# Shift and scale of the first three chunks computed by one-column matmuls in the start of a hybrid layer kernel

## The chip, the cores and the metric

The kernel runs on one core of a Trainium2 chip. Time is device time in microseconds (us) for one execution of the whole program. The engines are TensorE (PE; its weight loads are shown apart as PEld), VectorE (DVE), ScalarE (ACT), GpSimd (POOL) and SyncE (SP), which issues most of the transfers. Each engine runs its instructions strictly in the order of the program's listing for that engine, and they wait for each other through semaphores. The transfers named below are all issued from SP's one queue, at most eight of them outstanding.

## The reference

One layer on x of 1024 rows (S) by 1024 columns (D), in float32. The start, which the change touches, computes

```
c_act = silu(c)
mod   = c_act @ w_ada + b_ada          # 6 x 1024 columns
shift_t, scale_t, gate_t, shift_f, scale_f, gate_f = split(mod)
h     = x * (1 + scale_t) + shift_t
proj  = h @ w_in
```

The rest of the layer takes `proj` apart: a gated delta rule over 8 heads behind a short convolution, band attention over 16 heads, both projected and merged by gates, an output projection, a LayerNorm, then a second modulation, an up-projection, a convolution of width 3, a gated product, a down-projection and a second LayerNorm.

## The kernel before

Products of full precision are made of three products of the type fp32r: each operand is split into a high part (a cast) and a low part (the rest), and `hh·wh`, `hl·wh` and `hh·wl` are added up in one PSUM bank (`mm_fm`, L284). Plain float32 products, which the start uses too, run on TensorE as two passes, each a weight load and a multiply.

The program goes through a start stage, the delta-rule heads with the gates' projections between them, the attention, the branches' projections and the merge, the first LayerNorm, the up-projection (L1193, with fewer products by sums of blocks), the down-projection (L1497), and the last LayerNorm. A scheduler that simulates the engines decides the order of instructions on each engine; the source order of the calls is what it starts from. So a change in one place moves instructions in others.

The start stage makes h transposed, in 8 chunks of 128 of its columns, and multiplies each chunk at once with the first three blocks of weights of w_in (called k, g and q after what they produce):

- `ada_cols(j)` (L354 to L368) loads chunk j's 1024x128 columns of w_ada for the shift and for the scale, as four transfers of 256 KB in two tiles `wa`, then x's columns of the chunk (`load_x`, `xj`, 512 KB). On VectorE it multiplies each 128-row slab of w_ada by its entry of c_act (`csil`, one value a partition) and adds the eight up: `acc`, by one TENSOR_SCALAR (L363) and seven SCALAR_TENSOR_TENSOR (L365) of 128x256.
- On TensorE two products with a column of ones (L397, into `pmods`) add up acc over the partitions; ScalarE adds the bias (L400). That gives shift and scale as one value a partition.
- For each half of the rows: four transposes of x (L406) into one PSUM bank `px`; ScalarE makes h in float32 (L407) and its high part `hh` (L408) from it; GpSimd subtracts to the low part `hl` (L409).
- `dense_chunk` (L383) multiplies the chunk two behind the transposed one with the three weight blocks: 18 products of 512 columns a chunk.
- `first_weights` (L380) loads one weight block (`raw`, 512 KB, L185); ScalarE casts it to `wh` (L177), GpSimd subtracts to `wl` (L180).

Columns of two chunks ahead are loaded before the loop (`LEAD` is 2), k's weights behind chunk 0's loads and g's behind chunk 1's; q's come behind chunk 2's loads and three small loads (L344 to L350). When all chunks are multiplied, ScalarE takes the first finished product (L526) and the delta rule's first stage begins.

Of the kernel before, what the change touches and what calls it, by code (L numbers as in the profile page):

```python
# [12 lines left out]
ALU = mybir.AluOpType  # L13
# [4 lines left out]
P = 128  # L18
# [24 lines left out]
LAG0 = 2  # L43
PACC = 1
PTR = 0
G0 = 1
GA = (3, 2, 2, 2, 3, 2, 2, 99)
EP = (4,12)
# [105 lines left out]
def hybrid_layer(  # L154
# [182 lines left out]
        DVE.tensor_scalar(bb[:, :, m], vt[:, o:o + NK], float(m), None, ALU.add)  # L337

    pmods = pbank("pmods", "pm")
    accs, mark0 = {}, {}  # L340

    def ab_weights():
        raw = ring("rab", [P, NK, 16])
# [10 lines left out]
    def ada_cols(j):  # L354
        wa = [ring("wa", [P, 4, 2, P]) for _ in range(2)]
        for i in range(2):
            for m in range(2):
                SP.dma_start(wa[i][:, :, m, :],
                             w_ada2[4 * P * i:4 * P * i + 4 * P, m * D + j * P:m * D + j * P + P].rearrange(
                                 "(k p) n -> p k n", p=P))  # L360
        acc = accs[j] = ring("acc0", [P, 2, P])
        with tc.issue_after(mark0["acc"]) if mark0 and PACC else nullcontext():
            DVE.tensor_scalar(acc, wa[0][:, 0], csil[:, 0:1], None, ALU.mult)  # L363
            for k in range(1, NK):
                i = DVE.scalar_tensor_tensor(acc, wa[k // 4][:, k % 4], csil[:, k:k + 1], acc,  # L365
                                             ALU.mult, ALU.add)
        mark0["acc"] = i.ins
        return load_x(j)  # L368
# [9 lines left out]
    wfirst, pend = {}, {}  # L378

    def first_weights(m):  # L380
        wfirst[m] = wblock(kview(w_in2, first[m][0], P), NK)

    def dense_chunk(k):  # L383
        for m in first:
# [4 lines left out]

    xs = []  # L390
    for j in range(LEAD):
        xs.append(ada_cols(j))
        first_weights("kg"[j])
    for j in range(NK):
        pm = pmods[:, 2 * j:2 * j + 2]
        for m in range(2):
            PE.matmul(pm[:, m:m + 1], accs[j][:, m, :], ones[:, 0:1], start=True, stop=True)  # L397
        cs = ring("mc", [P, 2])
        for m in range(2):
            ACT.activation(cs[:, m:m + 1], pm[:, m:m + 1], AF.Identity, bias=bb[:, j, m:m + 1])  # L400
        h32 = ring("h32", [P, S])
        for n in range(2):
            N = slice(512 * n, 512 * n + 512)
            px = pbank(nm("px"), "px")
            for t in range(4):
                tr = PE.transpose(px[:, t * P:t * P + P], xs[j][:, 4 * n + t, :], ident)  # L406
            ACT.activation(h32[:, N], px, AF.Identity, bias=cs[:, 0:1], scale=cs[:, 1:2])  # L407
            ACT.activation(hh[:, j, N], px, AF.Identity, bias=cs[:, 0:1], scale=cs[:, 1:2])  # L408
            POOL.tensor_tensor(hl[:, j, N], h32[:, N], f(hh[:, j, N]), ALU.subtract)  # L409
        if j + LEAD < NK:  # L410
            xs.append(ada_cols(j + LEAD))
        if j == 0:
            wab, al, dtb = ab_weights()
            first_weights("q")
        if j == VJ:
            o = VO["b_gate"]
            vectors(o, [rows(b_gate[0]), rows(b_conv_ffn[0])])
            DVE.tensor_scalar(hbg, vt[:, o:o + 2 * NK], 0.5, None, ALU.mult)
            vectors(VO["conv_a"], [conv_a[0].rearrange("t (r p) -> (t r) p", p=P),
                                   norm_a, rows(ln1_g[0]), rows(ln1_b[0])])  # L420
            vectors(VO["conv_f"], [conv_ffn[0, 0:2].rearrange("t (r p) -> (t r) p", p=P)])
            vectors(VO["conv_f"] + 88, [rows(conv_ffn[0, 2])])
        if j >= LAG:
            with tc.issue_after(tr.ins) if PTR else nullcontext():
                dense_chunk(j - LAG)
# [1216 lines left out]
```

## Time and profile before

| | |
|---|---|
| median of 3 runs | 2221.73 us (2216.29 to 2221.82) |
| profiled execution | 2222.92 us |
| its span in the trace | 2221.2 us, granted TensorE clock 0.987 |
| busy: PE / DVE / ACT / POOL | 96% / 70% / 47% / 26% of the span |
| loads in the first 75 us | 32 of w_ada (256 KB), 8 of x and 6 of w_in (512 KB) |

A row of the timeline gives the start, the time, the engine, the source line, the operation, the output and inputs by the program's names, their shapes and a count; in brackets stands how long the engine was idle before it, and what ended that. Rows of the waits give engine, tile and line, what was waited for, and the sum, number and longest of the waits. A row of a group has the count, the busy time and the mean of one in ns, and the idle time before. The groups of one tile give the shortest, median and longest in ns. A line can be that of a helper that all engines' work of a kind shares (L177 and L180 split any operand).

### The profile page before, as it was taken

The page shows a single profiled execution, that of the slowest core. Times are in us where ns is not written, and L with a number is a line of the kernel's source. Part 1 is how long each engine was busy: PE and PEld are TensorE (multiplying, and loading weights), DVE is VectorE, ACT ScalarE, POOL GpSimd, SP SyncE. Part 2 cuts the span into 40 slices and gives each one's busy share as a digit, 9 for nine tenths or more (in the row PEclk, how much of TensorE's full clock was granted, in tenths as well). Part 3 has the DMA queues.
Part 4 walks back from the last instruction along what each step waited for, and adds up shares of the span by engine and source line. Part 5 has one row for each costly group of instructions (what it writes and reads, how often), then busy time and mean ns, then how long its engine had stood idle before and what let it go on. Part 6 is the DMA issues. An engine that isn't in the chain of part 4 may idle for free. (4 is left out here: it accounts for less than half of the span.)

```text
span 2221.2 us, 31629 instructions
## 1 busy us (share of the span) xinstructions
PE 2125.3 (96%) x11469; PEld 1776.9 (80%) x11469; DVE 1555.7 (70%) x3228; ACT 1037.9 (47%) x2216; POOL 588.5 (26%) x544
## 2 busy tenths in 40 slices
PE   6998999999999999999999999999899999999998
PEld 5687787777878787798989788888788878887876
DVE  8567585765667664467676653556998788879897
ACT  4645253434334334467675642235544444445453
POOL 4323232332322232233342522424011000000023
PEclk9999999999999999999999999999999999999999
DMA  9232333423233412211111424342242222253222
GB/s 286 80 112 78 91 94 107 119 74 108 85 91 93 142 36 82 79 57 51 60 55 65 154 91 137 105 152 86 67 161 95 86 76 83 89 209 133 95 95 86
DMA packets 228415, 224.68 MB, mean 101 GB/s; under 512 B 27482, under 2 KB 184595, under 8 KB 228259
## 3 DMA queue, kind: packets, MB, share of 16 engines
q1 hardware_dynamic: 228179, 222.63, 31.6%
q8 instruction: 90, 1.47, 0.3%
q14 instruction: 66, 0.54, 0.1%
q10 hardware_dynamic: 80, 0.03, 0.0%
HBM read 180.63 MB, written 48.28 MB: 103 GB/s over the span
## 5 line engine op out<-in xcount | busy, mean ns | idle before, releaser
L180 POOL TENSOR_TENSOR wl<-raw,wh 128x1024 fp32r<-128x1024 f32 x88 | 212.2, 2413 | 325.4 <-ACT wh L177 303.1
L1193 PE MATMUL pup<-hh,wop 128*128 128x512 f32 x704 | 225.2, 391 | 1.6 <-DVE wop L180 1.6
L1193 PE MATMUL pup<-t,wop 128*128 128x512 f32 x792 | 190.1, 393 | 3.3 <-ACT t L177 2.0
L1193 PEld LDWEIGHTS pup<-t,wop 128*128 128x128 f32 x792 | 148.2, 188 | 38.0 <-ACT t L177 2.4
L1193 PEld LDWEIGHTS pup<-hh,wop 128*128 128x128 f32 x704 | 132.0, 188 | 31.0 <-DVE wop L180 2.0
L177 ACT CAST wh<-raw 128x1024 fp32r<-128x1024 f32 x88 | 92.4, 1050 | 134.6 <-DMA raw<-in_w_in_dram 56.0
L1234 POOL TENSOR_TENSOR cc<-cc,G 128x512 f32<-128x512 f32 x22 | 44.6, 2028 | 375.9 <-DVE G L1216 311.7
L284 PE MATMUL pqkv<-hh,wh 128*128 128x512 f32 x352 | 143.1, 407 | 0.0
L284 PE MATMUL pqkv<-hl,wh 128*128 128x512 f32 x352 | 140.8, 400 | 0.0
L284 PE MATMUL pqkv<-hh,wl 128*128 128x512 f32 x352 | 139.8, 399 | 0.0
L1193 PE MATMUL pup<-hl,wop 128*128 128x512 f32 x352 | 137.5, 391 | 0.0
L663 DVE TENSOR_TENSOR FT<-FT,G 128x16 f32<-128x16 f32 (+30 forms) x248 | 120.9, 488 | 17.6 <-POOL G L608 10.3
L944 POOL TENSOR_SCALAR G<-G,FT 128x640 f32<-128x640 f32 (+4 forms) x103 | 69.9, 681 | 182.3 <-DVE FT L943 160.4
L177 ACT CAST wop<-wr 128x512 fp32r<-128x512 f32 x110 | 65.6, 620 | 99.1 <-DVE wr L1179 65.1
L284 PE MATMUL pgt<-hh,wl 128*128 128x512 f32 x240 | 95.1, 396 | 0.8 <-POOL wl L180 0.8
L284 PE MATMUL pgt<-hh,wh 128*128 128x512 f32 x240 | 95.4, 397 | 0.3 <-DVE tmp L530 0.3
L284 PE MATMUL pgt<-hl,wh 128*128 128x512 f32 x240 | 94.7, 395 | 0.0
L1497 PE MATMUL pdn<-hl 128*128 128x512 f32 x360 | 86.7, 395 | 3.9 <-DVE hl L180 2.4
L180 DVE TENSOR_TENSOR wop<-wr,wop 128x512 fp32r<-128x512 f32 x110 | 80.2, 733 | 13.3 <-ACT wop L177 12.4
L963 DVE TENSOR_TENSOR pl<-pp,ph 128x512 fp32r<-128x512 f32 (+2 forms) x116 | 72.5, 635 | 17.4 <-ACT ph L962 16.6
L1497 PEld LDWEIGHTS pdn<-hl 128*128 128x128 f32 x360 | 68.5, 191 | 19.2 <-DVE hl L180 2.8
L941 ACT ACTIVATE G<-G,FT 128x640 f32<-128x640 f32 (+4 forms) x103 | 71.6, 696 | 19.0 <-DVE FT L936 16.9
(457 smaller groups left out, 6127.8 us busy)
## 6 DMA issues: line engine op xcount, KB each, us to landing
raw<-in_w_in_dram SPq DMA_DIRECT2D x72, 512.0 KB
wr<-in_w_up_dram SPq DMA_DIRECT2D x44, 512.0 KB
raw<-in_w_ada_dram SPq DMA_DIRECT2D x32, 512.0 KB
dr<-g_d SPq DMA_DIRECT2D x18, 512.0 KB
dr<-in_w_down_dram SPq DMA_DIRECT2D x18, 512.0 KB
wa<-in_w_ada_dram SPq DMA_DIRECT2D x32, 256.0 KB
gates_d<-GT SPq DMA_DIRECT2D x32, 256.0 KB
g_d<-G SPq DMA_DIRECT2D x14, 512.0 KB
```

Source lines behind the costliest of these rows:

```text
L177: ACT.copy(h, src)
L180: return le.tensor_tensor(l, src, f(h), ALU.subtract).ins
L284: PE.matmul(ps, a[:, k, :], r[k][:, 512 * n:512 * n + 512], start=(k == 0 and a is wh and r is rh), stop=(k == NK - 1 and a is wl))
L663: DVE.tensor_tensor(pr[:, :, 0:i + 1], ft[:, :, 0:i + 1], fa[:, i:i + 1, 0:i + 1].to_broadcast([P, 8, i + 1]), ALU.mult)
L941: ACT.activation(sb[:, 0:n], sb[:, 0:n], AF.Exp, bias=mx[:, nb - 1:nb], scale=-1.0, accum_out=mx[:, 2:3])
L944: POOL.tensor_scalar(sb[:, 0:n], sb[:, 0:n], mx[:, 3:4], 0.0, ALU.mult, ALU.add)
L963: DVE.tensor_tensor(pl[:, B, :], pp, f(ph[:, B, :]), ALU.subtract)
L1193: PE.matmul(ps, a[:, u, k, :], b[v][k], start=(new and k == 0 and u == 0 and v == 0), stop=(k == 3 and u == 1), skip_group_check=not new)
L1234: self.later(7, lambda: POOL.tensor_tensor(o, o, self.t, ADD))
L1497: PE.matmul(sets[s_][i], a[:, u, i * P:i * P + P], b[:, v, :], start=(new and not seed and j == 0 and u == 0 and v == 0), stop=(j == len(q ...
```

## The change

For the first three chunks (`MP`) the sums on VectorE go. TensorE multiplies the slabs of w_ada out instead: slab k as the stationary operand, entry k of c_act as the one moving column, eight products for the shift and eight for the scale, accumulated in `pmods`. That is 48 products more (96 passes) and six products with ones fewer (12 passes). In the whole start stage, the low parts `hl` of the chunks and `wl` of the three first weight blocks are subtracted on VectorE instead of GpSimd. And the load of k's weights is called before chunk 0's columns, that of g's before chunk 1's.

```
+MP = 3
@@
-    accs, mark0 = {}, {}
+    accs, was, mark0 = {}, {}, {}
@@ ada_cols
+        was[j] = wa
+        if j < MP:
+            return load_x(j)
         acc = accs[j] = ring("acc0", [P, 2, P])
@@
     def first_weights(m):
-        wfirst[m] = wblock(kview(w_in2, first[m][0], P), NK)
+        wfirst[m] = wblock(kview(w_in2, first[m][0], P), NK, le=DVE)
@@
     for j in range(LEAD):
+        first_weights("kg"[j])
         xs.append(ada_cols(j))
-        first_weights("kg"[j])
     for j in range(NK):
         pm = pmods[:, 2 * j:2 * j + 2]
         for m in range(2):
-            PE.matmul(pm[:, m:m + 1], accs[j][:, m, :], ones[:, 0:1], start=True, stop=True)
+            if j < MP:
+
+                for k in range(NK):
+                    PE.matmul(pm[:, m:m + 1], was[j][k // 4][:, k % 4, m, :], csil[:, k:k + 1],
+                              start=(k == 0), stop=(k == NK - 1))
+            else:
+                PE.matmul(pm[:, m:m + 1], accs[j][:, m, :], ones[:, 0:1], start=True, stop=True)
@@
-            POOL.tensor_tensor(hl[:, j, N], h32[:, N], f(hh[:, j, N]), ALU.subtract)
+            DVE.tensor_tensor(hl[:, j, N], h32[:, N], f(hh[:, j, N]), ALU.subtract)
```

The scheduler also orders things anew. Below, numbers behind a name tell tiles of that name apart; they differ between the two programs.

ScalarE in the start, before: `wh_13` is the cast of g's weights, `wh_23` that of q's, `px_27` and `px_28` are the halves of a chunk's transposes; the first two px rows are chunk 1's first half and, behind the small L351, its second half.

```order
L177 CAST wh_13_161<-raw_15_163 128x1024
L400 ACTIVATE G_2_93<-pmods_122,G_2_93 128x1 x2
L407 ACTIVATE h32_26_221<-px_27_222,G_2_93 128x512
L408 ACTIVATE hh_84<-px_27_222,G_2_93 128x512
L351 ACTIVATE SB_1_92<-SB_1_92 128x8
L407 ACTIVATE h32_26_221<-px_28_230,G_2_93 128x512
L408 ACTIVATE hh_84<-px_28_230,G_2_93 128x512
L177 CAST wh_23_211<-raw_25_213 128x1024
```

ScalarE now, from chunk 0's first half (`px_17`) to chunk 1's first (`px_27`):

```order
L417 ACTIVATE h32_16_169<-px_17_170,G_2_93 128x512
L418 ACTIVATE hh_84<-px_17_170,G_2_93 128x512
L352 ACTIVATE SB_1_92<-SB_1_92 128x8
L178 CAST wh_23_201<-raw_25_203 128x1024
L417 ACTIVATE h32_16_169<-px_18_178,G_2_93 128x512
L418 ACTIVATE hh_84<-px_18_178,G_2_93 128x512
L410 ACTIVATE G_2_93<-pmods_122,G_2_93 128x1 x2
L417 ACTIVATE h32_26_225<-px_27_226,G_2_93 128x512
```

The cast of q's weights stood behind both halves of chunk 1; now it stands ahead of chunk 0's second half (`px_18`).

TensorE between the two halves of chunk 1's transposes, before: seven products with the weights of k (`wh_7`, `wl_8`) and g (`wh_13`).

```order
L406 MATMUL px_27_222<-ident_68,xj_12_159 128x128 x4
L284 MATMUL pfirst_39_292<-hh_84,wh_7_139 128x512
L284 MATMUL pfirst_40_299<-hh_84,wh_13_161 128x512
L284 MATMUL pfirst_40_299<-hl_85,wh_13_161 128x512
L284 MATMUL pfirst_41_300<-hh_84,wh_13_161 128x512
L284 MATMUL pfirst_39_292<-hl_85,wh_7_139 128x512
L284 MATMUL pfirst_39_292<-hh_84,wl_8_140 128x512
L284 MATMUL pfirst_41_300<-hl_85,wh_13_161 128x512
L406 MATMUL px_28_230<-ident_68,xj_12_159 128x128 x4
```

TensorE there now, with the three products ahead of the first half (`wh_23` and `wl_24` are q's weights, `wa_19` and `wa_20` chunk 2's slabs):

```order
L285 MATMUL pfirst_42_325<-hh_84,wh_23_201 128x512
L285 MATMUL pfirst_42_325<-hl_85,wh_23_201 128x512
L285 MATMUL pfirst_42_325<-hh_84,wl_24_202 128x512
L416 MATMUL px_27_226<-ident_68,xj_15_149 128x128 x4
L285 MATMUL pfirst_39_310<-hh_84,wh_4_123 128x512
L285 MATMUL pfirst_41_318<-hh_84,wh_10_137 128x512
L285 MATMUL pfirst_43_326<-hh_84,wh_23_201 128x512
L404 MATMUL pmods_122<-csil_109,wa_19_186 128x1 x4
L404 MATMUL pmods_122<-csil_109,wa_20_187 128x1 x4
L404 MATMUL pmods_122<-csil_109,wa_19_186 128x1 x4
L404 MATMUL pmods_122<-csil_109,wa_20_187 128x1 x2
L416 MATMUL px_28_234<-ident_68,xj_15_149 128x128 x4
```

Products with q's weights now stand ahead of chunk 1's transposes, and 14 of chunk 2's 16 one-column products between the halves.

VectorE now, in the middle of the stage: `h32_26` is chunk 1's h, `h32_32` chunk 2's, `h32_44` chunk 3's; `wa_47_354` and `wa_48_355` are the two tiles of chunk 5's columns, `wa_53_409` is the first of chunk 6's.

```order
L367 TENSOR_SCALAR G_2_93<-wa_47_354,csil_109 128x256
L419 TENSOR_TENSOR hl_85<-h32_26_225,hh_84 128x512
L369 SCALAR_TENSOR_TENSOR G_2_93<-wa_47_354,csil_109,G_2_93 128x256 x3
L369 SCALAR_TENSOR_TENSOR G_2_93<-wa_48_355,csil_109,G_2_93 128x256
L419 TENSOR_TENSOR hl_85<-h32_32_276,hh_84 128x512
L369 SCALAR_TENSOR_TENSOR G_2_93<-wa_48_355,csil_109,G_2_93 128x256 x3
L419 TENSOR_TENSOR hl_85<-h32_32_276,hh_84 128x512
L419 TENSOR_TENSOR hl_85<-h32_44_337,hh_84 128x512
L367 TENSOR_SCALAR G_2_93<-wa_53_409,csil_109 128x256
L369 SCALAR_TENSOR_TENSOR G_2_93<-wa_53_409,csil_109,G_2_93 128x256 x3
L419 TENSOR_TENSOR hl_85<-h32_44_337,hh_84 128x512
```

Before, no lower part of a chunk stood on VectorE; now they stand between the steps of later chunks' sums. On SP's queue the small vector loads (L314) and the next three weight blocks moved ahead of the second tile of chunk 5's columns or of the rest, and chunk 7's columns ahead of chunk 6's.

## The prediction

> **What bounds the kernel now.** I read the page's first part, then the busy time by stretches of the start, the waits there, and the timeline of single instructions.
>
> ```profile
> span 2221.2 us, 31629 instructions
> PE 2125.3 (96%) x11469; PEld 1776.9 (80%) x11469; DVE 1555.7 (70%) x3228; ACT 1037.9 (47%) x2216; POOL 588.5 (26%) x544
> ```
>
> TensorE is busy 96% of the span: over the whole program only its work and its waits count. The change touches the start alone, so that is read by itself (columns: stretch, its length, then busy time and instructions of PE, PEld, DVE, ACT and POOL, the granted clock, DMA share, GB/s).
>
> ```profile
> 0.00:21.50 21.50, 3.96 (x14) 2.85 (x14) 14.06 (x23) 7.19 (x12) 11.50 (x19) 1.00 0.95 273
> 20.00:23.00 3.00, 1.48 (x6) 1.38 (x7) 2.82 (x7) 0.41 (x2) 0.15 (x1) 1.00 0.41 49
> 24.00:26.00 2.00, 2.00 (x8) 1.61 (x7) 1.35 (x4) 1.45 (x3) 0.00 (x0) 1.00 1.15 345
> 26.00:43.00 17.00, 16.91 (x89) 13.91 (x88) 15.44 (x21) 9.41 (x18) 10.05 (x8) 1.00 1.15 343
> 43.00:45.00 2.00, 2.00 (x13) 1.61 (x12) 1.93 (x3) 1.13 (x2) 1.08 (x1) 1.00 0.24 62
> 45.00:49.00 4.00, 2.83 (x17) 2.19 (x16) 3.82 (x7) 1.59 (x5) 1.27 (x1) 1.00 0.90 255
> 49.00:56.00 7.00, 7.00 (x38) 5.62 (x37) 6.71 (x10) 4.08 (x8) 3.63 (x3) 1.00 1.06 309
> 58.00:66.00 8.00, 5.78 (x30) 3.43 (x30) 0.00 (x0) 2.29 (x6) 0.21 (x1) 1.00 0.01 3
> ...
> 73.40 0.69 ACT L526 ACTIVATE y<-pfirst,vt 128x512 f32<-128x512 f32 x1
> ```
>
> Three stretches: to 21.5 us TensorE waits for the first data and VectorE's sums; from then to 45 it is gapless, so what delays it there delays the end; from 45 to 66 it idles a little over 4 us in all (1.2 in 45 to 49, 2.2 in 58 to 66). The stage ends at 73.40, where ScalarE takes the first finished product. The waits that VectorE's sums cost TensorE:
>
> ```profile
> PE pmods L397 <- DVE G L365: 9.2, 4, 6.8
> PEld pfirst L284 <- POOL hl L409: 0.3, 1, 0.3
> ...
> 21.52 1.01 PE L397 MATMUL pmods<-ones,G 128*128 128x1 f32 x4 [6.78 <-DVE G L365]
> 46.99 0.61 PE L397 MATMUL pmods<-ones,G 128*128 128x1 f32 x4 [1.18 <-DVE G L365]
> 57.74 0.60 PE L397 MATMUL pmods<-ones,G 128*128 128x1 f32 x4 [0.98 <-DVE G L365]
> ```
>
> Of 9.2 us, 6.8 is chunk 1's wait before 21.52, which the change removes; the other two belong to chunks that keep their sums.
>
> **The change, step by step.** 1. *What replaces the 6.8 us.* After 21.52 the old order needs no q weights for some time: ScalarE casts them only behind chunk 1. In the new order the cast stands ahead of chunk 0's second half, on ScalarE's one queue, and TensorE's q products ahead of chunk 1's transposes. So the landing of the q weights decides.
>
> ```profile
> 19.97 0.43 SPq L185 DMA_DIRECT2D raw<-in_w_in_dram  x1
> 20.45 4.07 SPq L358 DMA_DIRECT2D wa<-in_w_ada_dram  x4
> ...
> 26.92 0.59 DVE L363 TENSOR_SCALAR G<-wa,csil 128x256 f32<-128x256 f32 x1 [1.53 <-DMA wa<-in_w_ada_dram]
> ```
>
> Chunk 3's first 512 KB of w_ada, right behind the q weights in the queue, ended a wait at 26.92. At 345 GB/s 512 KB take 1.5 us, so the q weights landed near 25.4. The change puts the same eleven blocks and the same three small loads ahead of them: I keep 25.4. The bounds: the data pause at 20 to 23 us (49 against 345 GB/s, 2.6 us, and some of the next) follows those small issues; without it 22.5; 26.9 at the latest. So the wait goes, and a later one takes its place.
>
> 2. *From the landing to chunk 1's second half.*
>
> ```profile
> 29.20 1.05 ACT L177 CAST wh<-raw 128x1024 fp32r<-128x1024 f32 x1
> 24.55 0.78 ACT L407 ACTIVATE h<-px,G 128x512 f32<-128x512 f32 x1 [1.56 <-PE px L406]
> 25.89 0.20 ACT L351 ACTIVATE SB<-SB 128x8 f32<-128x8 f32 x1
> 27.86 0.78 ACT L407 ACTIVATE h<-px,G 128x512 f32<-128x512 f32 x1 [1.76 <-PE px L406]
> L180 DVE TENSOR_TENSOR ob<-raw,ob 128x1024 fp32r<-128x1024 f32 x6 | 7.3, 1222 | 8.3 <-ACT ob L177 4.9 <-DMA ob_d<-ob 3.4
> 23.40 1.05 PE L406 MATMUL px<-ident,xj 128*128 128x128 f32 x4
> 25.96 0.63 PE L284 MATMUL pfirst<-hl,wh 128*128 128x512 f32 x1
> 26.39 0.63 PE L284 MATMUL pfirst<-hh,wl 128*128 128x512 f32 x1
> 29.50 0.40 PE L284 MATMUL pfirst<-hl,wh 128*128 128x512 f32 x1
> 29.74 0.39 PE L284 MATMUL pfirst<-hh,wl 128*128 128x512 f32 x1
> ```
>
> Cast 1.05: 26.45. Chunk 0's second half on ScalarE takes the 1.34 from 24.55 to 25.89: 27.8. Meanwhile VectorE subtracts the q low part: this shape costs it 1.22 on other tiles, to 27.7, and the third q product issues by 28.1. Chunk 1's transposes (1.05) end at 29.2. Three products follow. Products start 0.43 us apart at 26 us and 0.23 apart at 29.6, the granted clock being 1.00 in both rows: after 7 us of idling TensorE is slow, which that column doesn't show. It restarted at 21.52 and was fast between 26.39 and 29.5. In the new order it idles again until the cast at 26.45, so three products cost 1.3: 30.5.
>
> Then come 14 of chunk 2's 16 one-column products, each two passes of load and multiply: 28 passes. Before has such passes only with ones as moving column, in fours:
>
> ```profile
> 21.52 0.93 PEld L397 LDWEIGHTS pmods<-ones,G 128*128 128x128 f32 x4 [7.28 <-DVE G L365]
> 37.13 0.52 PEld L397 LDWEIGHTS pmods<-ones,G 128*128 128x128 f32 x4
> L397 PEld LDWEIGHTS pmods<-ones,G x32: 186/192/338, 9.9 to 58.1; 128*128 128x128 f32 x32
> 27.55 0.19 PEld L284 LDWEIGHTS pfirst<-hh,wh 128*128 128x128 f32 x1
> ```
>
> Less the last load's own time (0.338 slow, 0.19 fast), three steps take 0.59 and 0.33: 0.20 a pass slow, 0.11 fast. The first fast load stands at 27.55, 6.0 us after the restart; the last slow product 4.9 after. I take 6.0, so fast from 32.5: ten passes at 0.20, eighteen at 0.11, together 4.0, and 34.5. Chunk 1's second transposes (0.6) let ScalarE begin at 35.1, against 27.86: **+7.2**. Bounds of this term: 3.1 (all fast) to 5.6 us (all slow) for the 28 passes.
>
> The Trainium skill (TensorE: Matmul & The Clock Gate, Part 2, "LDWEIGHTS (loading the stationary operand)") prices a load by its columns over 1.2, in nanoseconds; for 128 that is 107 ns whatever the state, which agrees with the fast 0.11 and not with the slow 0.20. An estimate by that page is 28 x 0.107 = 3.0 us, and chunk 1's second half 1.0 earlier.
>
> 3. *What follows, to 73.40.* TensorE's remaining work is the same but for one product more done by then in the new order (twelve against eleven): −0.2. The waits of 1.18 and 0.98 should go, since TensorE comes 7 us later to the same sums: −2.2; they stay if the sums are as late (bound 0). Two new ones come from VectorE's queue, where a lower part stands behind a sum that waits for its data.
>
> ```profile
> L365 DVE SCALAR_TENSOR_TENSOR G<-wa,csil,G x56: 477/485/2506, 6.3 to 57.2; 128x256 f32<-128x256 f32 x56
> L180 DVE TENSOR_TENSOR hl<-dr,hl 128x512 fp32r<-128x512 f32 x54 | 35.9, 695 | 2.7 <-ACT hl L177 1.7 <-PE pdn L1497 1.0
> L409 POOL TENSOR_TENSOR hl<-h,hh 128x512 fp32r<-128x512 f32 x16 | 21.2, 1322 | 33.9 <-ACT hh L408 33.8
> L180 POOL TENSOR_TENSOR wl<-raw,wh 128x1024 fp32r<-128x1024 f32 x3 | 7.5, 2513 | 7.1 <-ACT wh L177 7.1
> ```
>
> Chunk 2's first lower part is queued behind chunk 5's fifth sum step. Its data is the tenth 512 KB after the q weights: 25.4 + 10 x 1.53 at 343 GB/s = 40.7, and the small vector loads, which before cost 1.6 of 43 to 45 and 1.0 of 45 to 49, now lie ahead of it: 43.4. With 0.5 for that step and 0.7 for the part it is ready at 44.6. TensorE wants it after 27 products of 0.23 and 20 passes of 0.1 to 0.11 from 34.8: near 43.0. So +1.6, bounds 0 (no pause) and 1.8. Behind it on VectorE wait the same chunk's second part and all later sums. Chunk 3's second part stands behind four steps of chunk 6's sum, whose data the new order of loads puts behind chunk 7's and three weight blocks: five blocks on, at 309 to 343 GB/s, near 51.4; with 1.9 for the steps and 0.7, 54.0 against TensorE's 52.6 to 53: +1.2, bounds 0 and 1.4. The last chunk's part takes VectorE 0.7 where it took GpSimd 1.3: −0.3 by the last product (−0.6 at most).
>
> The new waits end by the data, not by TensorE: up to 2.8 us more or less in step 2 is mostly taken up there.
>
> **The sum**: 7.2 − 0.2 − 2.2 + 1.6 + 1.2 − 0.3 = **+7.3 us**. Against the profiled execution (span 2221.2, with 1.7 around it 2222.9) that is 2230.2; that execution is 1.2 above the median, so on the median of 2221.7 I say **2229.0**.
>
> *Costed at nothing:* the 64 passes of chunks 0 and 1 (12.8 us at 0.20), the weights loaded ahead and the removed 24 sum steps: all lie before 25.4, under the wait for the q weights. If these landed at 22.5 the passes would still be done, w_ada of chunk 1 being the seventh block of twelve; were they not, each four cost 0.8. GpSimd's freed 28.7 us (21.2 + 7.5) buy nothing by themselves, its lower parts being waited for 0.3 us in sum; what they buy is VectorE's steps at 0.485 rather than up to 2.5 us, which is in the −2.2. After 73.40 the order differs in a few neighbouring rows, taken as zero.
>
> **Rivals.** *A: the pause in the data does not recur.* The q weights land at 22.5, TensorE restarts 2.9 earlier, and the rest goes as above: +4.4, **2226.1**. For it: the small loads' issue may overlap otherwise; against: it is the same queue in the same order.
>
> *B: TensorE stays slow through the one-column products*, which leave the array nearly empty. 28 passes at 0.20 cost 5.6 instead of 4.0, and some ten products after them at 0.43 instead of 0.23, 2.0: 3.6 more, **2232.6**, if the new waits stay as large because VectorE is late too; if their data comes as worked out, TensorE's lateness takes the place of their 2.8: 2229.8. For it: the fast pace came here after 5 us of 512-column work; against: fours of one-column passes stand amid it without harm. The Trainium skill (TensorE: Matmul & The Clock Gate, Part 4: PE-mode transpose) says that transposes do not count as TensorE's busy time for the clock gate; it says nothing of one-column products, and no row here shows one in a long run.
>
> *C, the other side: the delay is taken up again, and the kernel isn't slower.* Its place is 45 to 66 us, where TensorE idles 4.4 us in the old order; if all of that goes and neither new wait comes, the sum is 7.2 − 0.2 − 4.4 = +2.6, **2224.3**, and with A's landing −0.3, 2221.4. It decides if chunk 5's fifth step has its data by 41.7 and chunk 6's by 50.4 (the times TensorE wants the parts, less the steps). For it: 40.7 without the pause; against: the small loads stand ahead, and 2.2 of the idle time comes from ScalarE's last chunk, not from sums.
>
> That the change doesn't do what it says is out: the new order shows the products and the moved parts.
>
> **How the numbers follow.** My forecast 0.52, A 0.15, B 0.13, C 0.12, and 0.08 for a gain in rows after 73.40 that I can't see. My case's own range is 2226 to 2232: without the new waits −2.8, with the old ones kept +2.2. For 8 times in 10 it reaches into C and over B: 2220 to 2235. A measurement of this kernel tells 0.3% from no change, 6.7 us, so slower begins at 2228.4: three fifths of my case (0.31) and B, 0.44. Same: the rest of mine (0.21), A, and 0.11 of C, 0.47. Faster: the last 0.08 and 0.01 of C.
>
> **What would show it.** Right: ScalarE's q cast near 25.5, TensorE idle before it for 5 us or more, chunk 1's second half near 35, TensorE waiting for VectorE's lower parts near 43 and 53, the first finished product taken near 81. Wrong in step 1: the cast at 23; in step 2: chunk 2's passes 0.20 apart to their end; in step 3: no waits for lower parts. Wrong as a whole: ScalarE's first take at or before 76 us.

## The result, and the profile after

The changed kernel is slower by two thirds of a per cent.

| | before | after |
|---|---|---|
| median of 6 runs each | 2222.18 us (2216.29 to 2224.11) | 2234.76 us (2229.30 to 2238.34) |
| ratio, with its 95% interval | | 1.0065 (1.0053 to 1.0077) |
| profiled execution | 2222.92 us | 2233.64 us |
| first finished product taken | 73.40 us | 82.41 us |

The page's first part, after:

```profile
span 2231.9 us, 31777 instructions
PE 2146.4 (96%) x11553; PEld 1796.8 (81%) x11553; DVE 1543.5 (69%) x3223; ACT 1038.2 (47%) x2216; POOL 560.8 (25%) x525
```

TensorE is busy 21.1 us longer (2146.4 against 2125.3) in a span that is 10.7 us longer: it idles 10.4 us less and works 21.1 us more. A pass is one weight load and one multiply, two to each of the added products. The added passes are most of the 21.1 us (64 at 0.21 and 32 at 0.12 us, read below, make 17, less twelve that went); what is left is the same products done more slowly.

*Where the time goes, by stage.* The table gives, for each kernel's profiled execution, when TensorE begins the gates' products (soon after the start stage), and then the length of each later stage, between TensorE's first or last products of the neighbouring stages. "After, again" is the changed kernel's profiled execution beside a later group of runs; its median there was 2235.88 against 2219.50, a ratio of 1.0071 (1.0056 to 1.0086).

| | before | after | after, again |
|---|---|---|---|
| start, to the gates' first product | 80.6 | 89.5 (+8.9) | 89.9 (+9.3) |
| delta rule and gates | 550.0 | 552.9 (+2.9) | 552.4 (+2.4) |
| attention, branches | 737.7 | 739.1 (+1.4) | 742.1 (+4.4) |
| merge, up-projection | 615.2 | 615.2 | 615.0 |
| down-projection | 204.6 | 202.2 (−2.4) | 200.4 (−4.2) |

The start costs 9.0 us by the first finished product, and that repeats (82.80 again, +9.4). The rest of the +12.6 between the medians lies behind it.

*The start.* A dense product is one of the stage's 144 products of 512 columns; at the fast pace they start about 0.23 us apart, at the slow pace 0.43. Busy time by stretches, after; the columns are those of the prediction (PE, PEld, DVE, ACT, POOL, granted clock, DMA share, GB/s):

```profile
7.00:15.00 8.00, 7.55 (x36) 7.55 (x37) 1.59 (x3) 1.46 (x3) 0.00 (x0) 1.00 1.14 344
15.00:22.00 7.00, 7.00 (x36) 7.00 (x34) 0.92 (x2) 1.66 (x3) 0.46 (x1) 1.00 0.89 229
22.00:27.00 5.00, 4.96 (x13) 3.15 (x13) 1.51 (x3) 2.60 (x5) 0.00 (x0) 1.00 1.07 317
32.00:34.00 2.00, 2.00 (x12) 2.00 (x12) 1.89 (x5) 0.62 (x1) 0.00 (x0) 0.50 0.65 191
34.00:36.00 2.00, 2.00 (x5) 1.61 (x6) 1.41 (x3) 1.14 (x4) 0.00 (x0) 0.50 0.50 144
36.00:38.00 2.00, 2.00 (x6) 1.52 (x6) 0.15 (x1) 0.00 (x0) 0.00 (x0) 0.50 0.73 203
74.00:76.00 2.00, 2.00 (x7) 1.51 (x6) 0.10 (x1) 1.42 (x2) 0.00 (x0) 0.50 0.00 0
```

And the timeline and the waits of the same kernel:

```profile
15.19 5.54 PE L404 MATMUL pmods<-csil,wa 128*128 128x1 f32 x26
24.40 1.05 ACT L178 CAST wh<-raw 128x1024 fp32r<-128x1024 f32 x1 [3.58 <-DMA raw<-in_w_in_dram]
29.05 3.34 PE L404 MATMUL pmods<-csil,wa 128*128 128x1 f32 x28
33.38 0.78 ACT L417 ACTIVATE h<-px,G 128x512 f32<-128x512 f32 x1 [3.42 <-PE px L416]
37.41 0.63 PE L285 MATMUL pfirst<-hh,wl 128*128 128x512 f32 x1
37.84 0.63 PE L285 MATMUL pfirst<-hh,wh 128*128 128x512 f32 x1
39.65 0.60 PE L416 MATMUL px<-ident,xj 128*128 128x128 f32 x4
44.02 0.48 DVE L369 SCALAR_TENSOR_TENSOR G<-wa,csil,G 128x256 f32<-128x256 f32 x1 [3.78 <-DMA wa<-in_w_ada_dram]
45.16 0.50 PE L285 MATMUL pfirst<-hl,wh 128*128 128x512 f32 x1 [0.91 <-DVE hl L419]
51.60 0.35 DVE L367 TENSOR_SCALAR G<-wa,csil 128x256 f32<-128x256 f32 x1 [2.10 <-DMA wa<-in_w_ada_dram]
54.17 0.50 PE L285 MATMUL pfirst<-hl,wh 128*128 128x512 f32 x1 [0.73 <-DVE hl L419]
82.41 0.69 ACT L536 ACTIVATE y<-pfirst,vt 128x512 f32<-128x512 f32 x1
```

Read in order of time:

- From 7 us on TensorE is full, not waiting: the 64 passes of chunks 0 and 1 stand where it idled before. They run at the slow pace, 26 in 5.54 us, 0.21 each, although the granted clock reads 1.00. The 6.8-us wait is gone, and so is the idle time that I expected ahead of the cast at 24.40.
- Chunk 2's 28 passes run fast (3.34 us, 0.12 each). But as they end, near 31.9 us, the granted clock falls to 0.50. It stays there to about 38.8 and catches what stands behind them: dense products are 0.43 us apart at 37.4. Twelve of them, and the transposes and passes ahead, lose about 3 us (worked out against wide80 below).
- Chunk 2's first transposes come at 39.65, 9.7 us behind their place before (about 2 us of that are nine dense products more that are done by then, 27 against 18):

```profile
29.97 0.60 PE L406 MATMUL px<-ident,xj 128*128 128x128 f32 x4
```

- The waits for chunk sums near 47 and 58 us are gone; in their place stand the two waits for VectorE's lower parts, 0.91 and 0.73.
- At the stage's end, at 74 to 76 us, the granted clock is 0.50 again.

*Behind the start.* One wait of TensorE's is new, 330 us later. Its row, after and before, and the transfers on SP's queue and VectorE's step that it hangs on:

```profile
413.72 0.50 PE L285 MATMUL pgt<-hh,wh 128*128 128x512 f32 x1 [3.74 <-DVE tmp L540]
401.91 3.11 SPq L612 DMA_DIRECT2D fa_d<-am  x4
410.75 2.27 DVE L673 TENSOR_TENSOR FT<-FT,G 128x16 f32<-128x16 f32 x1 [2.66 <-POOL G L618]
```

```profile
399.72 0.50 PE L284 MATMUL pgt<-hh,wh 128*128 128x512 f32 x1 [0.25 <-DVE tmp L530]
391.39 1.82 SPq L602 DMA_DIRECT2D fa_d<-am  x4
398.83 0.18 DVE L663 TENSOR_TENSOR FT<-FT,G 128x16 f32<-128x16 f32 x1 [1.26 <-POOL G L608]
```

All is 10.5 us later up to the four issues; these take 1.3 us longer, GpSimd's step behind their data is later, VectorE waits for that 1.4 us longer and then takes 2.1 us longer over one small product, and TensorE waits 3.5 us more. Again TensorE's wait was 3.52 us. Why four issues take 3.11 rather than 1.82 us isn't known. The longer product, 2.27 us for 128x16, has company: GpSimd's step of 128x1024, after and before,

```profile
410.63 2.35 POOL L646 TENSOR_TENSOR y<-y,tmp 128x1024 f32<-128x1024 f32 x1
```

```profile
399.32 2.38 POOL L636 TENSOR_TENSOR y<-y,tmp 128x1024 f32<-128x1024 f32 x1 [0.53 <-PE pq L630]
```

now runs beside it, and the two end together (413.02 and 412.98). Before, GpSimd's step came 0.3 us behind VectorE's, which took 0.18; there VectorE's next one, at 399.96, took 1.78 us and ended with GpSimd's, at 401.7. So being 1.4 us late put VectorE's step behind the start of GpSimd's.

### The profile page after: what moved, and what is told of

It is laid out like the page before. It is cut to its first block, busy times and chain, and to the rows that moved or that the text cites. A ratio compares the mean times of both kernels' runs of the same rounds, so it can differ in the third digit from the quotient of the medians.

```text
span 2231.9 us, 31777 instructions
## 1 busy us (share of the span) xinstructions
PE 2146.4 (96%) x11553; PEld 1796.8 (81%) x11553; DVE 1543.5 (69%) x3223; ACT 1038.2 (47%) x2216; POOL 560.8 (25%) x525
## 5 line engine op out<-in xcount | busy, mean ns | idle before, releaser
L181 POOL TENSOR_TENSOR wl<-raw,wh 128x1024 fp32r<-128x1024 f32 x85 | 204.6, 2410 | 325.7 <-ACT wh L178 295.3
L673 DVE TENSOR_TENSOR FT<-FT,G 128x16 f32<-128x16 f32 (+30 forms) x248 | 122.4, 494 | 19.8 <-POOL G L618 12.6
```

Source lines behind the costliest of these rows:

```text
L181: return le.tensor_tensor(l, src, f(h), ALU.subtract).ins
L673: DVE.tensor_tensor(pr[:, :, 0:i + 1], ft[:, :, 0:i + 1], fa[:, i:i + 1, 0:i + 1].to_broadcast([P, 8, i + 1]), ALU.mult)
```

## The experiments

Three theories were at stake for the start. **The clock**: long runs of one-column products leave TensorE at the slow pace, and the dense products behind them pay for it (the prediction's rival B). **VectorE's queue**: the lower parts, moved behind sums that wait for data, hold TensorE, and so the end of the stage goes by the data. **The data**: what the new order of loads puts ahead of chunk 5's and chunk 6's columns. They can be true together, each as a limit behind the next.

"First" is the time at which ScalarE takes the first finished product in the profiled execution, and what that is against 73.40. The median stands against that of before on the same chip.

| run | first, us | median − before, us | ratio (95%) |
|---|---|---|---|
| mp0 | 69.68 (−3.7) | +2.8 | 1.0020 (1.0007 to 1.0033) |
| mp1 | 75.61 (+2.2) | +3.6 | 1.0013 (0.9996 to 1.0031) |
| mp2 | 78.64 (+5.2) | +5.9 | 1.0031 (1.0019 to 1.0044) |
| the change (again) | 82.80 (+9.4) | +16.4 | 1.0071 (1.0056 to 1.0086) |
| mp3only | 89.75 (+16.4) | +19.4 | 1.0082 (1.0062 to 1.0102) |
| wide80 | 82.25 (+8.9) | +18.2 | 1.0088 (1.0067 to 1.0110) |
| hlpool | 83.91 (+10.5) | +17.2 | 1.0077 (1.0061 to 1.0094) |
| widehlpool | 86.20 (+12.8) | +21.8 | 1.0091 (1.0076 to 1.0106) |
| loads | 81.44 (+8.0) | +14.1 | 1.0057 (1.0039 to 1.0075) |
| wideloads | 84.22 (+10.8) | +10.0 | 1.0042 (1.0027 to 1.0057) |
| clean | 83.43 (+10.0) | +11.4 | 1.0055 (1.0034 to 1.0077) |
| wideclean | 78.20 (+4.8) | +6.2 | 1.0027 (1.0011 to 1.0044) |
| hldve | 73.67 (+0.3) | −0.3 | 0.9997 (0.9987 to 1.0007) |
| mp0nole | 72.23 (−1.2) | −6.0 | 0.9973 (0.9958 to 0.9989) |

### How many chunks: mp0, mp1, mp2, and the products alone

The number of chunks that TensorE multiplies out, all else of the change kept:

```
-MP = 3
+MP = 0          (mp1: 1, mp2: 2)
```

> The changed kernel with MP = 0: all sums on VectorE as before, but lower parts of the start on VectorE and the first weights loaded ahead. Clock theory: no long run of one-column products, so no slow stretch beyond that before 27 us; the q weights' cast is again behind chunk 1's first half. The first finished product is taken between 72 and 76, the whole is 2219 to 2226, about the kernel before. Order-and-data theory (VectorE's queue with lower parts behind sums is what costs): the waits for lower parts remain and it is 2228 to 2234.

> The changed kernel with MP = 1: only chunk 0 by one-column products; ScalarE's cast of the q weights is behind both halves of chunk 0. Both theories: the run of sixteen is over by 11 us and hurts nothing; the cast stands before chunk 1's first half. Order-and-data theory, whose cost lies in the cast: 2226 to 2230, 4 to 8 us over the kernel before. Clock theory: 2220 to 2226.

> The changed kernel with MP = 2: chunk 2's sixteen products go back to sums on VectorE, the order of the weight cast stays. Clock theory: the drop to 0.50 at 32 us is gone (it followed chunk 2's run), the slow stretch of 22 to 27 us stays; first finished product near 78, whole 2228 to 2231. Order-and-data theory: as the changed kernel less the 3 to 4 us of chunk 2's passes only if nothing waits behind them, so 80 to 82 us and 2231 to 2235.

The first finished product comes at 69.68, 75.61, 78.64 and 82.41 us with 0, 1, 2 and 3 chunks: each chunk costs 3 to 6 us, and without any the rest of the change is a gain of 3.7 us in the start. So the delay belongs to the one-column products and the order that the scheduler makes for them, not to the lower parts or the loads as such. mp2, without chunk 2's passes, has no fall of the clock near 32 us, as the clock theory expected: the granted clock is 1.00 to 41.8, where it falls behind a wait of 2.66 us for a lower part. But mp0 shows that a half-clock stretch needs no such run of passes: there the clock falls within a wait of 1.78 us and is 0.50 from 22.7 to 29.5 us, and mp0 is the earliest of the four all the same.

The end does not follow one for one: mp0 leads by 3.7 us at its first product and is 2.8 us behind at the end. In mp0 and mp1 the scheduler also put the attention in another order, and in the profiled executions the stage of attention and branches took 741.7 and 744.6 us against 737.7. That may be the cause, but it isn't shown: the changed kernel, whose order there is nearer the old one, had 739.1 and 742.1.

The reverse, the products without the rest (lower parts on GpSimd, k's and g's weights behind the chunks' columns as before):

```
-    wfirst[m] = wblock(kview(w_in2, first[m][0], P), NK, le=DVE)
+    wfirst[m] = wblock(kview(w_in2, first[m][0], P), NK)
-    DVE.tensor_tensor(hl[:, j, N], h32[:, N], f(hh[:, j, N]), ALU.subtract)
+    POOL.tensor_tensor(hl[:, j, N], h32[:, N], f(hh[:, j, N]), ALU.subtract)
     for j in range(LEAD):
-        first_weights("kg"[j])
         xs.append(ada_cols(j))
+        first_weights("kg"[j])
```

> The one-column products alone (MP = 3) on the kernel before: loads of the first weights and lower parts as before. Clock and load-order theories: TensorE slow until about 27 and at a granted 0.50 after chunk 2's products, chunk 5's and 6's w_ada late; first finished product 80 to 84, and the order of the attention changes too: whole 2232 to 2240. If the moved lower parts or loads were the cause of the loss: 73 to 76 and 2220 to 2226.

The first product comes at 89.75, 16.4 us later than before and later than either theory had it. Here chunk 2's passes stay slow to their end; the timeline of this kernel has

```profile
28.41 4.26 PE L404 MATMUL pmods<-csil,wa 128*128 128x1 f32 x20
58.96 1.01 PE L407 MATMUL pmods<-ones,G 128*128 128x1 f32 x4 [2.99 <-DVE G L369]
```

that is 0.21 a pass at 28 us, and later a wait of 2.99 us for a sum. The other parts of the change take back 7 us of what the products cost.

### The clock against VectorE's queue

wide80 gives each pass 80 equal moving columns instead of one. The order on TensorE and ScalarE is that of the changed kernel, and VectorE's too up to 56 us (behind that, three lower parts stand one step later); a pass's weight load is the same.

```
-    PE.matmul(pm[:, m:m + 1], was[j][k // 4][:, k % 4, m, :], csil[:, k:k + 1],
+    PE.matmul(wide[m], was[j][k // 4][:, k % 4, m, :],
+              csil[:, k:k + 1].to_broadcast([P, 80]),
```

> The changed kernel with the same order on every engine, but each of the 48 products has 80 equal moving columns instead of one (the entry of c_act repeated; only the first result column is used, so the computation is the same). Clock theory (one-column products leave the array nearly idle, so TensorE stays slow through chunks 0 and 1 and drops to a granted 0.50 near 32 us): the products now count as work, the granted clock is 1.00 from 28 to 39 us, dense products start 0.23 apart in place of 0.43, chunk 2's first half is reached at least 3 us sooner than 40.3, ScalarE takes the first finished product near 78 to 79 in place of 82.4, and the whole is 3 to 5 us under the changed kernel (2230 or so). Order-and-data theory (the late weight cast and VectorE's queue set it all): nothing moves, 82 to 83 us and 2234 to 2236.

Busy time by stretches and the waits of wide80:

```profile
32.00:34.00 2.00, 2.00 (x13) 1.74 (x12) 1.93 (x5) 1.75 (x4) 0.00 (x0) 1.00 0.79 233
34.00:36.00 2.00, 2.00 (x11) 1.59 (x10) 1.64 (x4) 0.00 (x0) 0.00 (x0) 1.00 0.13 36
35.92 0.60 PE L418 MATMUL px<-ident,xj 128*128 128x128 f32 x4
39.88 0.50 PE L285 MATMUL pfirst<-hl,wh 128*128 128x512 f32 x1 [2.33 <-DVE hl L421]
45.81 0.80 PE L285 MATMUL pfirst<-hl,wh 128*128 128x512 f32 x1 [2.80 <-DVE hl L421]
82.25 0.69 ACT L538 ACTIVATE y<-pfirst,vt 128x512 f32<-128x512 f32 x1
```

The granted clock now stays at 1.00 where it was 0.50, TensorE does eleven instructions in 34 to 36 us where it did five, and chunk 2's first transposes come 3.7 us earlier (35.92 against 39.65). From chunk 1's second transposes to these it takes 4.32 us (31.60 to 35.92) where the changed kernel took 7.40 (32.25 to 39.65): the fall of the clock costs 3.1 us there. The passes of chunks 0 and 1 are slow with 80 columns too (32 in 7.12 us). But the first finished product is where it was: the lead is given back in two waits for VectorE's lower parts, 2.33 and 2.80 us, each behind a sum that waits for its data, and the granted clock falls behind the second (0.50 at 46 to 49 us). Two limits lie close behind one another, and the clock's delay covered the second.

If so, the lower parts on GpSimd, where no sum stands ahead of them, should free it:

```
-    DVE.tensor_tensor(hl[:, j, N], h32[:, N], f(hh[:, j, N]), ALU.subtract)
+    POOL.tensor_tensor(hl[:, j, N], h32[:, N], f(hh[:, j, N]), ALU.subtract)
```

hlpool is this in the changed kernel, widehlpool with the 80 columns as well; the changed kernel itself was run again beside them.

> The changed kernel with only the lower parts of h back on GpSimd (the order of loads is the same; the one-column products, the weights' lower parts on VectorE and the loads ahead stay). Two-limits theory (TensorE's stretch at half clock after the one-column run, and VectorE's lower parts queued behind sums that wait for data; either hides the other): TensorE's waits of 0.9 and 0.7 us for lower parts go, the granted 0.50 near 32 to 38 us stays, chunk 2 is reached near 40 as before, first finished product at 80 to 82, whole 2231 to 2234. Queue-alone theory (the wide products changed nothing because the clock costs nothing): first product at 76 to 78, whole 2226 to 2229.

> Both: 80 equal moving columns in place of one, and the lower parts of h on GpSimd. Two-limits theory: chunk 2 is reached near 36.6, no wait for lower parts of 2 us or more between 37 and 46, first finished product at 74 to 77 in place of 82.4, whole 2223 to 2229, 5 us or more under either single edit. Queue-alone theory: the same as with the lower parts on GpSimd alone. Clock-alone theory: the same as the wide products alone, 82 and 2234 to 2238.

> The changed kernel itself, once more, for a second profile. If what the start shows is fixed by the program, the same: TensorE slow to 27, granted 0.50 from 32 to 38.7, first finished product at 82 to 83, 2233 to 2236. If the half-clock stretches come by chance, their places and the first product move by several us.

Again has the stretch where it was, granted 0.50 from 32.6 to 39.4 us. hlpool has not, though its passes have one column and its order on TensorE is the changed kernel's up to 56 us:

```profile
27.29 0.60 PE L416 MATMUL px<-ident,xj 128*128 128x128 f32 x4
28.43 3.18 PE L404 MATMUL pmods<-csil,wa 128*128 128x1 f32 x28
35.80 0.60 PE L416 MATMUL px<-ident,xj 128*128 128x128 f32 x4
32.00:36.00 4.00, 4.00 (x22) 3.36 (x22) 3.79 (x8) 1.75 (x4) 1.41 (x1) 1.00 0.61 179
```

Chunk 2 is reached at 35.80, as early as with 80 columns, where the two-limits theory had it near 40. What differs is when TensorE became fast. In hlpool the transposes ahead of the passes, at 27.29, take 0.60 us, the fast time; in the changed kernel they take 1.06 at 27.36, and the products behind them are fast from about 28.5. The 3.4 us from there to the fall at 31.9 hold little but one-column passes; in hlpool about one and a half microseconds of fast transposes and dense products (26.95 to 28.43) stand ahead of the same passes. So a run of 28 such passes is not enough by itself.

Over all runs with three chunks: with one column, the clock fell at 31 to 33 us in three profiles (the changed kernel twice, and loads below), TensorE became fast only near 41 us in two (mp3only, and clean below), and in hlpool neither happened; with 80 columns, in none of four. So the moving columns bear on the clock, but what decides in one execution is not shown, and hlpool and widehlpool are no test of the two limits together, since in both the clock held to 47 us.

Both came out later at the first product, at 83.91 and 86.20. TensorE now waits for something else; hlpool, then widehlpool:

```profile
47.22 0.99 PE L407 MATMUL pmods<-ones,G 128*128 128x1 f32 x4 [4.18 <-DVE G L369]
```

```profile
47.50 0.98 PE L409 MATMUL pmods<-ones,G 128*128 128x1 f32 x4 [4.19 <-DVE G L369]
```

That is chunk 5's own sum. In TensorE's order its product with ones stands behind 48 of the stage's 144 dense products, as in the changed kernel; before, behind 72. So the data of chunk 5 stop TensorE whichever engine makes the lower parts, and behind 4.2 us of idling it is slow again (granted 0.59 over 46 to 52 us in hlpool). As a test of VectorE's queue this failed: taking the lower parts out of the queue changed what is waited for, not the wait.

### The loads

Then the data must come earlier. loads issues chunk 0's to chunk 7's columns in order, each behind the one before, and the next three weight blocks behind them; wideloads has the 80 columns too.

```
+    with tc.issue_after(lastld[-1]) if lastld else nullcontext():
         SP.dma_start(wa[i][:, :, m, :], ...
+    with tc.issue_after(lastld[-1]) if lastld else nullcontext():
+        ld = SP.dma_start(xj, ...
+    lastld.append(ld.ins)
```

> The changed kernel with the loads chained: chunk 5's, 6's and 7's columns in that order, ahead of the next stage's three weight blocks (which the scheduler had put between them). Load-order theory (after the wide products alone and the lower parts on GpSimd alone gained nothing: what holds the second half of the start is that chunk 5's and 6's w_ada land at 44 and 52 to 55, behind other loads): TensorE's waits of 0.9 and 0.7 us go, the half-clock stretch from 32 stays and is now what sets the pace; first finished product near 80, whole 2230 to 2233. If loads don't matter: 82 to 83 and 2234 to 2236.

> The chained loads and the 80 equal moving columns together. Load-order theory with the clock theory: TensorE reaches chunk 2 near 36.5 and isn't held for more than 1 us before 60; first finished product at 75 to 78 in place of 82.3 with the wide products alone, whole 2225 to 2230, so that the clock's 3 to 4 us show only when the loads are mended. If the two do not add: 80 to 82.

loads gained about 1 us at the first product (81.44 against 82.41 and 82.80), and nothing that shows at the end. wideloads still waits for the lower parts, 2.19 and 2.42 us, and its first product comes no earlier (84.22), though its median is 4.1 us under that of loads (2231.40 against 2235.52; four runs each, 2229.87 to 2232.20 and 2230.81 to 2236.56). The first product of one profiled execution and the end do not go together here:

```profile
39.75 0.50 PE L289 MATMUL pfirst<-hl,wh 128*128 128x512 f32 x1 [2.19 <-DVE hl L428]
45.30 0.60 PE L289 MATMUL pfirst<-hl,wh 128*128 128x512 f32 x1 [2.42 <-DVE hl L428]
38.74 0.35 DVE L372 TENSOR_SCALAR G<-wa,csil 128x256 f32<-128x256 f32 x1 [2.99 <-DMA wa<-in_w_ada_dram]
```

Chunk 5's first data still end a wait at 38.74 (37.85 in the changed kernel, where the same step stands). What is left ahead of them in the queue is the small vector loads. clean and wideclean hold those back as well, behind the columns, and ask for them a chunk later:

```
+    with tc.issue_after(lastld[-1]) if lastld and eng is SP else nullcontext():
         eng.dma_start(v[r:r + n, :], s_)
-    if j == VJ:
+    if j == 6:
```

These two have the same order on every engine and differ in the moving columns alone.

> The chained loads, and behind them the eight small vector loads too (their call moved one chunk on), with one-column products: all of the chunks' columns come without a pause. Load theory: chunk 5's two tiles land near 35 and 38 to 40 instead of 38 and 43, VectorE is never held for more than 1 us between 35 and 48, TensorE's waits for lower parts go; the half-clock stretch from 31 to 38 stays and sets the pace. First finished product 78 to 80, whole 2229 to 2233. If the loads don't matter: 81 to 82.

> The same order on every engine and the same loads, with 80 equal moving columns in place of one. Clock theory, now with nothing behind it to take the lead back: granted clock 1.00 from 28 to 58 us, chunk 2 reached near 36, no wait over 1 us; first finished product 3 to 4 us sooner than with one column (74 to 77), whole 3 us or more under it. If another queue takes the lead back again: the same first product as with one column.

clean, then wideclean:

```profile
30.00:34.00 4.00, 4.00 (x21) 4.00 (x20) 3.82 (x9) 0.38 (x1) 0.00 (x0) 1.00 1.13 335
29.91 5.97 PE L412 MATMUL pmods<-csil,wa 128*128 128x1 f32 x28
42.64 0.60 PE L424 MATMUL px<-ident,xj 128*128 128x128 f32 x4
83.43 0.69 ACT L544 ACTIVATE y<-pfirst,vt 128x512 f32<-128x512 f32 x1 [1.17 <-PE pfirst L289]
```

```profile
30.00:34.00 4.00, 4.00 (x31) 3.74 (x30) 3.81 (x9) 1.75 (x4) 0.00 (x0) 1.00 1.12 333
28.46 3.25 PE L413 MATMUL pmods<-csil,wa 128*128 128x80 f32 x28
35.87 0.60 PE L426 MATMUL px<-ident,xj 128*128 128x128 f32 x4
78.20 0.69 ACT L546 ACTIVATE y<-pfirst,vt 128x512 f32<-128x512 f32 x1 [1.17 <-PE pfirst L289]
```

With the data out of the way the pace has its price: 28 passes take 5.97 us with one column and 3.25 with 80, chunk 2's transposes are 6.8 us apart, the first finished product 5.2 us (83.43 against 78.20), and the medians 5.1 us (2232.44, five runs from 2230.00 to 2237.01, against 2227.29, ten runs from 2220.93 to 2234.66). So in this pair about 5 us are the clock's, once nothing else hides them. For the changed kernel that is not the size: there the same passes ran fast and the fall cost about 3 us, while clean's TensorE was slow without a break until about 41 us. Whether clean's other executions were slow as well is not on record. Nor do 80 columns always gain at the end: against its own partner, the median less that of before changed by +1.8 us (wide80), +4.6 (widehlpool), −4.1 (wideloads) and −5.2 (wideclean). wideclean's remaining 4.8 us at the first product, among them one wait of 1.18 us for a lower part, are not taken apart further. clean itself gained nothing that can be told over the change: its TensorE has no wait between 28 and 75 us, and at that pace earlier data were not needed.

### What of the change helps

hldve takes one part alone into the kernel before: the chunks' lower parts on VectorE, no one-column products, weights as before.

```
-    POOL.tensor_tensor(hl[:, j, N], h32[:, N], f(hh[:, j, N]), ALU.subtract)
+    DVE.tensor_tensor(hl[:, j, N], h32[:, N], f(hh[:, j, N]), ALU.subtract)
```

> The kernel before with one part of the change alone: the lower parts of h on VectorE instead of GpSimd (sums on VectorE for all chunks, loads and weights' lower parts as before). With MP = 0 the first product was taken at 69.7 instead of 73.4. If that gain comes from the lower parts on VectorE (sums no longer slowed beside GpSimd, 0.7 us instead of 1.3 for the last part): 70 to 72, and the whole 2216 to 2220, at most 4 us under the kernel before. If it comes from the weights loaded ahead: 73 to 74 and 2219 to 2222.

No difference: 73.67 at the first product, 0.9997 at the end. The lower parts on VectorE cost and gain nothing by themselves in this kernel, where the sums are all on VectorE too.

mp0nole adds the weights loaded ahead to that; the weights' own lower parts stay on GpSimd.

```
-MP = 3
+MP = 0
-    wfirst[m] = wblock(kview(w_in2, first[m][0], P), NK, le=DVE)
+    wfirst[m] = wblock(kview(w_in2, first[m][0], P), NK)
```

> The kernel before with the loads of the first weights ahead and the lower parts of h on VectorE, without one-column products and with the weights' lower parts on GpSimd; the order behind the start is nearly that of before. With MP = 0 the first product came 3.7 us sooner than before, but the order of the attention had changed and took it back. Theory that the later order took it back: first product at 69 to 71, whole 2214 to 2218, faster than both kernels. Theory that any gain in the start is lost later: 2219 to 2223.

This one beats both: 2215.43 against 2221.43, 0.9973 (0.9958 to 0.9989). At the first finished product it leads by 1.2 us only. The rest is not located: the execution that was profiled took 2222.04 us, the longest of ten (2210.13 to 2222.04), and shows no gain.

## Why the prediction was wrong

The likeliest of three, no change that can be measured, had 0.47; slower had 0.44. The time, 2234.76, is 5.8 us above the 2229.0 named and just inside the range.

**The landing of the q weights** (step 1): right. The cast began at 24.40, a microsecond before the 25.4 named.

**"… so fast from 32.5"** (step 2): wrong, and this is the step that failed in the start. The sum has TensorE idle until the cast, slow for 6.0 us behind it, and from then on fast for good. It did not idle: the 64 passes of chunks 0 and 1, costed at nothing, filled its time to 22.6 us at the slow pace, and nine dense products followed. Costing these passes at nothing was nearly right, for the third q product could not start before its weights' lower part was there (25.49 + 1.23 = 26.72, and it started at 26.77). TensorE was fast from about 28.5 us, so that chunk 1's second half came at 33.38 (+5.5) where 35.1 (+7.2) was named, and chunk 2's passes took 3.34 rather than 4.0. What the sum put at nothing is a fall of the pace once it is fast: near 31.9 us the granted clock fell to 0.50 for 6.8 us, which cost 3.1 us. Rival B had the mechanism (one-column products do not keep TensorE fast) with 0.13; it put 1.6 us of its cost in the passes, which ran fast, and 2.0 in ten products behind them, where twelve products and the transposes lost 3.1. In clean the passes were slow as B had it, 0.21 each; in hlpool nothing of B happened.

**The waits** (step 3): the two of before went, the two for VectorE's lower parts came, near 45.2 and 54.2 us, where 43 and 53 were named. The data came as worked out, at 44.02 and 51.60 us (43.4 and 51.4 were named). The waits were 0.91 and 0.73 rather than 1.6 and 1.2, since TensorE came to them at 44.25 and 53.44, behind the half clock, rather than at 43.0 and about 52.8. What the prediction said of them, that they end by the data and take up what TensorE is early or late, held best in wide80: there TensorE came sooner and waited 2.80 us for the same part, and 2.33 for the one ahead of it.

**The tail of the stage**: −0.3 was named. It was a loss: two microseconds at half the clock, 74 to 76 us, cost 1 us by themselves, by an estimate from the two paces.

**The first finished product**: 82.41 against "near 81"; +9.0 against +7.3. That the sum comes so close is in part luck: −1.7 (chunk 1's second half) and −1.2 (the new waits) made up for most of +3.1 (the half clock) and +1.3 (the tail). So the start explains 1.7 of the 5.8 us, and 0.5 are the kernel before, whose median was 2222.18 here and 2221.73 in the prediction.

**"After 73.40 … taken as zero"**: wrong, and in size the larger failure: +3.6 us on medians (12.6 − 9.0; the ratio of 1.0065 makes the whole 14.4 us, and this 5.4). The wait at 413.72 is one part: it recurs in all ten profiles of kernels with three chunks (3.1 to 4.4 us), and in none of mp2, mp1, mp0, hldve, mp0nole and before. The stage of the delta rule took 551 to 554 us in those with three chunks and 548 to 553 in the others. The rest can't be told from chance: the same stages in the same order differ by several microseconds from one execution to the next (attention and branches 739.1 and 742.1 us in two executions of the changed kernel), and the kernel before lost 2 to 4 us in the down-projection of its profiled execution that the changed kernel did not lose. So the profiled spans, 10.7 us apart, understate the difference, and the medians carry it. What part of the 3.6 us is the wait, and what makes its four issues longer, stays open.

**The other rivals**: A (weights at 22.5) and C (the delay taken up between 45 and 66 us) did not happen: the cast came at 24.40, and of C's two conditions the second failed, since both new waits came.

## What to carry to other kernels

Work put on an engine "in its idle time" can have a price behind it if it changes the pace at which that engine goes on. Here weight loads with one moving column filled TensorE's time, and in five profiles of six TensorE fell to the slow pace behind them or never left it; with 80 columns, where chunk 2's passes take the same 0.12 us, in none of four. Before costing such work at nothing, ask at what pace it runs and at what pace it leaves the engine, and look at more than one execution, since the same order of passes kept the pace in one profile. And a limit that is removed shows the next one: try both cures together (here the columns and the order of the loads) before either is called useless. Last, a term "taken as zero" far behind the edit was the larger part of the miss.

## What was unexpected of the hardware

A pass with one moving column keeps PE and PEld busy in the profile all the time (7.00 of 7.00 us at 15 to 22 us), and yet the granted clock fell to 0.50 at the end of 28 of them, near 31.9 us; in the same order with 80 columns it kept 1.00 there. The Trainium skill (TensorE: Matmul & The Clock Gate, "Part 4: PE-mode transpose") says that transposes don't count as TensorE's busy time in the same way as products; it says nothing of one-column products. The changed kernel is as if that held for them too; hlpool, where the clock held behind the same 28 passes, leaves the rule open.

The half clock lasted from about 31.9 to 38.8 us in the profile after, 6.8 us, and TensorE had been fast for about 3.4 us ahead of it. The same page's "Part 1: The HAM clock gate (the 'warmup' mystery)" puts the gate's window at about 3.4 us, with the half or the full rate and nothing between; the trace agrees, with one such window fast and two at half.

The granted clock reads 1.00 from the start until its first recorded change, whatever the pace: in clean it is 1.00 over 30 to 34 us while a pass takes 0.21 us. The pace is read from the steps between like instructions, not from that column.

A VectorE product of 128x16 took 2.27 us beside a GpSimd step of 2.35 us and ended with it; the same product took 0.18 us with none beside it.
